# A hybrid attention and state-space layer: padded key tiles, wider tap and sample visits, a sample's keys as 96 + 96 + 80 rows

## The chip, the cores and the metric

The kernel runs as one program on one core of a Trainium2 chip. The metric is the device time in microseconds (us) of one execution, from a program that is launched once; lower is better. The core has five engines that run their own instruction streams and meet at semaphores: TensorE (PE in the profile, with its weight loads apart as PEld), VectorE (DVE), ScalarE (ACT), GpSimd (POOL) and SyncE (SP), which here issues all the transfers, on one queue in order.

## What is computed

One layer works on 512 new rows of a prompt and on 8 running streams ("samples") of 16 new rows each, with 256 cached keys a stream. Both branches read the same normed input through one combined projection; cut to what matters here:

```python
h = rmsnorm(x, g) @ w_in                       # 640 rows x 1024, w_in 1024 x 8192
q, k, v, ga, u, gs, gl = split(h)
# attention: 8 heads, two softmax maps a head, q/k 64 wide, v 128 wide
s = einsum('bqmhd,bkmhd->bmhqk', q, k) - slopes * |q_pos - k_pos|     (masked by chunks of 64)
p = softmax(s);  w = p[:, 0] - lam * p[:, 1]
o = einsum('bhqk,bkhe->bqhe', w, v)            # samples: keys = 256 cached + 16 new
ya = (rmsnorm(o) * silu(ga)) @ w_attn_proj
# S5 state space: 64 groups of 16 channels, 64 complex states a group
hr, hi = associative_scan(a, b @ u)            # h[t] = a h[t-1] + b u[t], along the rows
ys = gelu(Re(c h) + d u);  ys = ys * sigmoid(ys @ w_glu + b_glu)
ys = (ys * silu(gs)) @ w_ssm_proj
y = x + (sigmoid(g_a) * ya + sigmoid(g_s) * ys) @ w_out
```

The new keys and values, and the last states, are outputs too.

## The kernel before, in words

Nearly all instructions are recorded at line 222, where `Meter.go` calls the engine; the rows are therefore told apart by the names of their tiles.

**The main line** is 4032 products into the banks `ps_mm`, in the order of the table `ORDER`: vA, u, kA, ga, qA, gs, kB, qB, vB, the rest of gs, xa, xs, then ap, gl, sp, o0 and o1. Each fp32 operand is split into a high and a low part of a faster type, and a product is done as hi x hi, hi x lo and lo x hi (`mm3`). Weights come in as `wraw` tiles of 512 KB and are split by ACT (`whi`) and DVE (`wlo`). Half A of the keys and queries serves heads 0 to 3, half B heads 4 to 7.

**Side work** is written as generators. The class `Weave` keeps a modelled clock of every engine, and puts the next step of a generator between two products of the main line when it expects its inputs to be there. This fixes PE's order at build time (`manual_schedule` for TensorE); the other engines' orders come from a list scheduler with its own model. On the chip every engine works in that order and waits at semaphores. A run of such instructions between two `ps_mm` products is called a visit here.

The side work that the change touches, in the order in which it runs:

- `ssm_tap`: for each of 16 blocks of four groups, DVE or POOL builds a table `E` and PE makes four products of 32 columns of the array (`ps_pv<-E,bbs`) into one bank. ACT and DVE evacuate it to `tap`, and SP writes it to `tap_d` in DRAM.
- `attend`: 16 steps for each half, four tiles of 128 queries by four heads, two score maps each, so 64 maps. A map is two products into `ps_s`: `kT,qT` on 128 rows (the query's hi and lo rows against the key's hi rows, which stand twice), and `kTl,qT` on the 64 rows of the head (the query's hi rows against the key's lo rows). All heads of a half share the tile `kTl`, one head of a pair in its rows 0 to 63, the other in rows 64 to 127. Then come transposes of the weights `sb` and products with the values (`ps_pv<-vt,wth` and `wtl`).
- `states`: the recurrence over chunks, in two parts of 45 and 44 columns through one buffer `R`. A part is loaded from `s_d` (4 transfers), runs step by step (four operations a step, `m`, `m`, `m`, `R`, on POOL or, in some steps, on DVE), and is stored to `r_d` (4 transfers). The second part cannot be loaded before the first is stored. `states` starts after the last tap (`after("tap")`), because its pool takes the taps' place, and its end (`after("states")`) opens the pool of the samples' scores.
- `evac_k` and `evac_q` norm the rows of keys and queries. The root (`rs`) is done on POOL, between the steps of `states`; PE transposes the result (`ps_tp<-ident,kn`), and DVE and ACT split it.
- `sample_setup`, `sample_k`, `sample_scores`: after `states`, the samples' cached keys `skt` (512 KB each, `KH` = 2 buffers) and the queries `qk` are loaded, `prep` copies the queries into the block-diagonal tiles `qbd`, and each sample gets two visits of four products of 32 columns (`ps_s<-skt,qbd`), one for each map.
- `sample_v`, `sample_pv`: the weights of a sample are transposed in pieces of 128, 128 and 16 keys, and multiplied with two value tiles `svt` (`VH` = 4 buffers) and a small one, `svn`, of 16 new rows.

`director` starts these in turn; the state-space outputs (`out_load` to `out_gelu`) and the last products follow.

Of the kernel before, what the change touches and what calls it, by code (L numbers as in the profile page):

```python
# [10 lines left out]
F32 = mybir.dt.float32  # L11
# [20 lines left out]
# columns of the packed parameters  # L32
# [27 lines left out]
    # of the two engines for plain arithmetic, the one with less to do  # L60
# [7 lines left out]
    # when the last part of what is read is there  # L68
# [9 lines left out]
    # when the n-th next tile of the tag has its place  # L78
# [4 lines left out]
    # when the place of a tile is free  # L83
# [34 lines left out]
    # the step goes on when its loads are there  # L118
# [70 lines left out]
class Meter:  # L189
    """An engine whose instructions are counted at their expected price."""  # L190
# [4 lines left out]
    def __getattr__(self, op):  # L195
        fn = getattr(self.e, op)

        def go(out, *args, **kw):
# [36 lines left out]
def trunk(nc, tc, a):  # L235
# [24 lines left out]
    # when the n-th result of the name is expected; with placed, as soon as its instructions are in  # L260
# [15 lines left out]
    # ---------------------------------------------------------------- helpers  # L276
# [22 lines left out]
    # when the n-th next bank is free  # L299
# [5 lines left out]
    # ---------------------------------------------------------------- DRAM scratch  # L305
# [5 lines left out]
    qk_d = [dram.tile([128, 8, 2, 2, 32], F32, name=f"qk_d{i}") for i in range(2)]   # row, sample, map, half  # L311
# [5 lines left out]
    # ---------------------------------------------------------------- constants  # L317
# [6 lines left out]
    isl = pers.tile([128, 2, 8], F32, name="isl")       # one over the slopes, by half, map and head  # L324
# [5 lines left out]
    # operands of the products: hi and lo parts, by k  # L330
# [6 lines left out]
    # ---------------------------------------------------------------- products  # L337
# [15 lines left out]
    # the transfers run two ahead of the splitting  # L353
# [1262 lines left out]
```

## Time and profile before

| what | value |
|---|---|
| three runs | 911.86, 914.41, 915.0 us; median 914.41 |
| profiled execution, span | 910.4 us (its own time is not listed apart) |
| PE | 874.9 us busy, 96% of the span |
| PEld | 778.4 us, 85% |
| DVE | 561.4 us, 62% |
| ACT | 377.8 us, 41% |
| POOL | 258.1 us, 28% |
| DMA | 165.78 MB, mean 182 GB/s |
| mean granted TensorE clock | 0.979 of full speed |

A row of a timeline gives start, duration, engine, operation with its tiles, shape and count, and in brackets the idle time before it with the one that ended it. A PE row's duration is from issue to result, and products overlap, so what a product costs PE is the distance from its start to the next start. For `64*128 64x384` read: 64 rows and 128 columns of the array, 384 elements streamed.

### The profile page before, as it was taken

The page shows a single profiled execution, that of the slowest core. Times are in us where ns is not written, and L with a number is a line of the kernel's source. Part 1 is how long each engine was busy: PE and PEld are TensorE (multiplying, and loading weights), DVE is VectorE, ACT ScalarE, POOL GpSimd, SP SyncE. Part 2 cuts the span into 40 slices and gives each one's busy share as a digit, 9 for nine tenths or more (in the row PEclk, how much of TensorE's full clock was granted, in tenths as well). Part 3 has the DMA queues.
Part 4 walks back from the last instruction along what each step waited for, and adds up shares of the span by engine and source line. Part 5 has one row for each costly group of instructions (what it writes and reads, how often), then busy time and mean ns, then how long its engine had stood idle before and what let it go on. Part 6 is the DMA issues. An engine that isn't in the chain of part 4 may idle for free.

```text
span 910.4 us, 15615 instructions
## 1 busy us (share of the span) xinstructions
PE 874.9 (96%) x5692; PEld 778.4 (85%) x5692; DVE 561.4 (62%) x1263; ACT 377.8 (41%) x796; POOL 258.1 (28%) x428
## 2 busy tenths in 40 slices
PE   8999998999999999789999999999899999999998
PEld 6898978899778788577777797889899999999986
DVE  6689278987596874467668843323577755565421
ACT  6332244554265443144556543433465644432110
POOL 2843076661124971497822110000000000000000
PEclk8999998999999999799999999999999999999999
DMA  8265647767439339553387579955989754345331
GB/s 297 98 204 160 199 143 216 232 209 237 125 105 200 100 97 142 122 163 92 104 151 261 162 257 356 352 186 177 278 239 306 259 205 154 99 130 173 105 126 58
DMA packets 145437, 165.78 MB, mean 182 GB/s; under 512 B 49104, under 2 KB 109136, under 8 KB 145360
## 3 DMA queue, kind: packets, MB, share of 16 engines
q1 hardware_dynamic: 145360, 164.78, 60.5%
q8 instruction: 45, 0.74, 0.3%
q14 instruction: 32, 0.26, 0.1%
HBM read 117.63 MB, written 42.93 MB: 176 GB/s over the span
## 4 chain that ended last, share of the span: by engine, by line
PE 69%; DMA 10%; DVE 9%; POOL 6%; issue 3%; ACT 2%; SPq 1%; ACTq 0%; DVEq 0%; POOLq 0%
PE ps_mm L222 55%; PE ps_s L222 7%; PE ps_tp L222 4%; PE ps_pv L222 3%; DMA wraw<-in_wb_dram 3%; POOL m L222 2%; DMA T<-tap_d 2%; DVE wlo L222 2%; SPq L222 1%; DMA R<-s_d 1%; DMA r_d<-R 1%; POOL rs L222 1%; DMA Ef<-e_d 1%; POOL R L222 1%; POOL F L222 1%
## 5 line engine op out<-in xcount | busy, mean ns | idle before, releaser
L222 PE MATMUL ps_mm<-xh,whi 128*128 128x320 f32 x640 | 207.8, 325 | 2.1 <-DVE ue L222 2.1
L222 PE MATMUL ps_mm<-xh,wlo 128*128 128x320 f32 x640 | 200.4, 313 | 0.0
L222 PE MATMUL ps_mm<-xl,whi 128*128 128x320 f32 x640 | 200.2, 313 | 0.0
L222 DVE TENSOR_TENSOR wlo<-wraw,whi 128x1024 fp32r<-128x1024 f32 x96 | 119.7, 1248 | 80.8 <-ACT whi L222 79.8
L222 ACT ACTIVATE whi<-wraw 128x1024 fp32r<-128x1024 f32 x96 | 101.6, 1059 | 123.7 <-PE ps_mm L222 94.7
L222 PEld LDWEIGHTS ps_mm<-xh,whi 128*128 128x128 f32 x640 | 122.8, 192 | 11.7 <-issue 8.6
L222 PEld LDWEIGHTS ps_mm<-xl,whi 128*128 128x128 f32 x640 | 122.9, 192 | 0.2
L222 PEld LDWEIGHTS ps_mm<-xh,wlo 128*128 128x128 f32 x640 | 122.5, 191 | 0.0
L222 PE MATMUL ps_mm<-whi,xh 128*128 128x512 f32 x240 | 100.6, 419 | 1.1 <-ACT xh L222 1.1
L222 PE MATMUL ps_mm<-wlo,xh 128*128 128x512 f32 x240 | 96.0, 400 | 0.0
L222 PE MATMUL ps_mm<-whi,xl 128*128 128x512 f32 x240 | 95.8, 399 | 0.0
L222 POOL TENSOR_TENSOR m<-a,R 128x64 f32<-128x64 f32 (+1 forms) x128 | 55.1, 455 | 13.6 <-DMA R<-s_d 6.5
L222 PEld LDWEIGHTS ps_mm<-whi,xh 128*128 128x128 f32 x240 | 46.5, 194 | 11.7 <-issue 1.4
L222 PEld LDWEIGHTS ps_mm<-whi,xl 128*128 128x128 f32 x240 | 46.3, 193 | 10.6 <-DVE xl L222 0.3
L222 PEld LDWEIGHTS ps_mm<-wlo,xh 128*128 128x128 f32 x240 | 46.4, 194 | 8.8 <-DVE wlo L222 0.7
L222 POOL TENSOR_TENSOR rs<-ss,mhalf 128x8 f32<-128x8 f32 x20 | 33.5, 1674 | 55.4 <-DVE ss L222 51.8
L222 PE MATMUL ps_mm<-ogh,whi 128*128 128x320 f32 x128 | 41.3, 323 | 0.0
L222 PE MATMUL ps_mm<-ogh,wlo 128*128 128x320 f32 x128 | 40.0, 313 | 0.0
L222 PE MATMUL ps_mm<-ogl,whi 128*128 128x320 f32 x128 | 39.9, 312 | 0.0
L222 PE MATMUL ps_mm<-yh,whi 128*128 128x320 f32 x128 | 39.6, 309 | 0.0
L222 PE MATMUL ps_mm<-yh,wlo 128*128 128x320 f32 x128 | 39.6, 309 | 0.0
L222 PE MATMUL ps_mm<-y2h,whi 128*128 128x320 f32 x128 | 39.6, 309 | 0.0
(291 smaller groups left out, 1897.0 us busy)
## 6 DMA issues: line engine op xcount, KB each, us to landing
wraw<-in_wb_dram SPq DMA_DIRECT2D x64, 512.0 KB
wraw<-in_wa_dram SPq DMA_DIRECT2D x32, 512.0 KB
u<-u_d SPq DMA_DIRECT2D x16, 640.0 KB
skt<-in_ckt_dram SPq DMA_DIRECT2D x16, 512.0 KB
svt<-in_cv_dram SPq DMA_DIRECT2D x16, 512.0 KB
u_d<-ue SPq DMA_DIRECT2D x8, 640.0 KB
gate_xa<-gate SPq DMA_DIRECT2D x16, 320.0 KB
e_d<-E SPq DMA_DIRECT2D x16, 256.0 KB
```

Of the source, the lines that this page charges most:

```text
L222: r = fn(out, *args, **kw)
```

## The change

Four parts. (a) The lo product of a score map is done on all 128 rows, with one lo tile for each head of a pair, whose other 64 rows are zero; POOL clears these rows, two memsets of 64 x 2048 in each half. (b) The taps of four blocks are built first, and then done in one visit of 16 products into one bank of 512 columns, with one evacuation by ACT. (c) The two score maps of a sample are done in one visit, with `KH` = 4 key buffers. (d) A sample's 272 keys are cut into 96, 96 and 80 rows; the last tile takes 64 cached and the 16 new ones, with `VH` = 6 buffers. All comments are gone too, and the program is built with `dynamic_dma_scratch_size=256`. The diff, cut to the core:

```diff
@@ ssm_tap
+        tpz = tpe.tile([128, TB, 240], F32, name="tap")
-            E = tpe.tile(sh, F32, name="E", tag="E", bufs=1)
+                E = tpe.tile(sh, F32, name="E", tag="E", bufs=TB)
...
-            yield room("pv")
+                yield room("pv") if b == b0 + TB - 1 else None
             pt = ps_pv()
-            for g in range(4):
-                PE.matmul(pt[g * 32:g * 32 + 32, :128], bbs[:, 4 * b + g:4 * b + g + 2, :].rearrange("p g n -> p (g n)"),
-                          Ef[:, g, :128], start=True, stop=True)
-            AC.activation(tp, pt[:, :128], AF.Copy)
+            for i, Ef in enumerate(Efs):
+                for g in range(4):
+                    gb = 4 * (b0 + i) + g
+                    PE.matmul(pt[g * 32:g * 32 + 32, i * 128:i * 128 + 128],
+                              bbs[:, gb:gb + 2, :].rearrange("p g n -> p (g n)"), Ef[:, g, :128], start=True, stop=True)
+            AC.activation(tp, pt[:, :TB * 128].rearrange("p (b c) -> p b c", b=TB), AF.Copy)
...
+            for i in range(TB):
+                SP.dma_start(tap_d[b0 + i].rearrange("n g c -> g n c"), tpz[:, i, :])
@@ evac_k
-                KT[hf] = [atk.tile([128, 4, 512], F32R, name=f"kT{x}", tag="kT", bufs=3) for x in "01l"]
+                KT[hf] = [atk.tile([128, 4, 512], F32R, name=f"kT{x}", tag="kT", bufs=4) for x in ("0", "1", "l0", "l1")]
+            if t == 0:
+                for h2 in range(2):
+                    PL.memset(f(KT[hf][2 + h2][HALVES[1 - h2]]), 0.0)
...
-                    split(d[own, :, ts], KT[hf][2][own, :, ts], pt[own])
+                    split(d[own, :, ts], KT[hf][2 + h2][own, :, ts], pt[own])
@@ attend
-            PE.matmul(ps[:, :nk], q[rows, j, :], kl[rows, j, :nk], start=False, stop=True)
+            PE.matmul(ps[:, :nk], q[:, j, :], kl[:, j, :nk], start=False, stop=True)
@@ sample_v
-        for x in range(16):
-            b, j = divmod(x, 2)
+        for x in range(24):
+            b, j = divmod(x, 3)
+            n = 96 if j < 2 else 64
+            SP.dma_start(v[:n], a["cv"][b, j * 96:j * 96 + n, :])
+            if j == 2:
+                SP.dma_start(v[64:80], v_d[b * 16:b * 16 + 16])
@@ sample_scores
+            yield Free(both(after("kh", 2 * b + 2), after("qbd", b + 1), room("s", 2)))
+            pss = [ps_s(), ps_s()]
             for m in range(2):
-                yield Free(both(after("kh", 2 * b + m + 1), after("qbd", b + 1), room("s")))
...
-                W.give("kh")
+            W.give("kh", 2)
@@ sample_pv
-            for j in range(2):
-                PE.transpose(ps[:, j * 128:(j + 1) * 128], w[:, j * 128:(j + 1) * 128], ident)
-            PE.transpose(ps[:16, 256:384], w[:, 256:272], ident)
+            for j, n in enumerate(VROWS):
+                PE.transpose(ps[:n, j * 128:(j + 1) * 128], w[:, j * 96:j * 96 + n], ident)
...
-            for j, x in enumerate((wt[:, 0], wt[:, 1], wn)):
+            for j, n in enumerate(VROWS):
                 v = VS.pop((b, j))
@@ constants
+VROWS = 96, 96, 80
+TB = 4
-KH = 2
-VH = 4
+KH = 4
+VH = 6
```

The planner and the scheduler answer to this with other orders. On POOL, where `states` passes from its first part to its second (`last` holds the column between them; `osc` and `rs` are roots for norms; kTl are the new lo tiles), the order before is:

```order
L222 TENSOR_TENSOR R<-R,m_4164 128x64
L222 COPY last<-R 128x64
L222 COPY R<-last 128x64
L222 TENSOR_TENSOR m_4321<-a_111,R 128x64
L222 TENSOR_TENSOR m_4322<-a_111,R 128x64
L222 TENSOR_TENSOR m_4321<-m_4321,m_4322 128x64
L222 TENSOR_TENSOR osc<-oss,mhalf 128x4
L222 TENSOR_TENSOR R<-R,m_4321 128x64
L222 TENSOR_TENSOR m_4327<-a_111,R 128x64
L222 TENSOR_TENSOR m_4328<-a_111,R 128x64
L222 TENSOR_TENSOR rs<-ss,mhalf 128x8
```

and with the change, with the two memsets some 20 rows further up, inside the first part:

```order
L222 TENSOR_TENSOR osc<-oss,mhalf 128x4
L222 TENSOR_TENSOR m_3986<-m_3986,m_3987 128x64
L222 MEMSET kTl_4344 64x2048
L222 MEMSET kTl_4345 64x2048
L222 TENSOR_TENSOR R<-R,m_3986 128x64
...
L222 COPY last<-R 128x64
L222 TENSOR_TENSOR osc<-oss,mhalf 128x4
L222 COPY R<-last 128x64
L222 TENSOR_TENSOR m_4256<-a_111,R 128x64
L222 TENSOR_TENSOR m_4257<-a_111,R 128x64
L222 TENSOR_TENSOR m_4256<-m_4256,m_4257 128x64
L222 TENSOR_TENSOR rs<-ss,mhalf 128x8
```

The first `rs` of half B moved from behind the first step that needs the loaded `R` to ahead of it, and the memsets of half B stand among the steps of `states`.

On SP's queue, where the samples' loads are issued once `states` is done (`skt` is 512 KB; `qk<-qk_d_70` are the queries, `qk<-qk_d_71` the new keys), the order before is:

```order
L222 DMA bias_s<-in_bias_s_dram 128x272
L222 DMA qk<-qk_d_71 128x128
L222 DMA skt<-in_ckt_dram 128x4x256 x2
L222 DMA qk<-qk_d_70 128x128 x2
L222 DMA v_d<-v 128x512
```

and with the change:

```order
L222 DMA bias_s<-in_bias_s_dram 128x272
L222 DMA qk<-qk_d_71 128x128
L222 DMA skt<-in_ckt_dram 128x4x256 x2
L222 DMA qk<-qk_d_71 128x128
L222 DMA skt<-in_ckt_dram 128x4x256 x2
L222 DMA qk<-qk_d_70 128x128 x2
```

The first queries stand behind four key loads in place of two.

On PE, the first visit of the samples' scores, before (ahead of it are 1906 products of the main line):

```order
L222 MATMUL ps_mm<-xh_94,whi 128x320
L222 MATMUL ps_mm<-xl_96,whi 128x320
L222 MATMUL ps_mm<-xh_94,wlo 128x320
L222 MATMUL ps_s<-skt,qbd_5501 32x272 x4
L222 MATMUL ps_pv<-vt,wth 128x256
L222 MATMUL ps_pv<-vt,wtl 128x128
```

and with the change (ahead of it are 1870):

```order
L222 MATMUL ps_pv<-vt,wth 128x256
L222 MATMUL ps_pv<-vt,wtl 128x128
L222 MATMUL ps_s<-skt,qbd_5330 32x272 x8
L222 MATMUL ps_mm<-xh_94,whi 128x320
L222 MATMUL ps_mm<-xl_96,whi 128x320
```

The visit holds eight products in place of four, and it stands 36 main products earlier. On the same engine the transposes of half B's second key tile moved from the place behind 1576 main products to that behind 1558.

## Rows read from the trace of the kernel before

**Rows 1.** The page: busy time by engine, and the chain by engine.

```profile
PE 874.9 (96%) x5692; PEld 778.4 (85%) x5692; DVE 561.4 (62%) x1263; ACT 377.8 (41%) x796; POOL 258.1 (28%) x428
...
PE 69%; DMA 10%; DVE 9%; POOL 6%; issue 3%; ACT 2%; SPq 1%; ACTq 0%; DVEq 0%; POOLq 0%
```

**Rows 2.** Timeline of PE, two score maps: start, us, operation.

```profile
301.92 0.39 PE L222 MATMUL ps_s<-kT,qT 128*128 128x384 f32 x1
302.24 0.44 PE L222 MATMUL ps_s<-kTl,qT 64*128 64x384 f32 x1
302.61 0.44 PE L222 MATMUL ps_s<-kT,qT 128*128 128x384 f32 x1
```

**Rows 3.** Timeline of PE, a visit of taps.

```profile
263.28 0.40 PE L222 MATMUL ps_mm<-whi,xl 128*128 128x512 f32 x1
263.60 0.42 PE L222 MATMUL ps_pv<-E,bbs 128*32 128x128 f32 x8
263.96 0.50 PE L222 MATMUL ps_mm<-whi,xh 128*128 128x512 f32 x1
264.30 0.40 PE L222 MATMUL ps_mm<-wlo,xh 128*128 128x512 f32 x1
264.54 0.40 PE L222 MATMUL ps_mm<-whi,xl 128*128 128x512 f32 x1
```

**Rows 4.** Timeline of PE, two visits of sample scores.

```profile
518.85 1.12 PE L222 MATMUL ps_s<-skt,qbd 128*32 128x272 f32 x16
519.90 0.42 PE L222 MATMUL ps_mm<-xh,whi 128*128 128x320 f32 x1
...
524.04 0.67 PE L222 MATMUL ps_s<-skt,qbd 128*32 128x272 f32 x8
524.64 0.41 PE L222 MATMUL ps_mm<-xh,whi 128*128 128x320 f32 x1
```

**Rows 5.** PE's waits: us in total, times, longest.

```profile
PE ps_tp L222 <- DVE kn L222: 9.0, 2, 6.7
```

**Rows 6.** Timeline of POOL, the chain of the states.

```profile
287.09 0.66 POOL L222 TENSOR_TENSOR m<-a,R 128x64 f32<-128x64 f32 x2 [6.52 <-DMA R<-s_d]
...
331.01 1.01 POOL L222 TENSOR_TENSOR osc<-oss,mhalf 128x4 f32<-128x4 f32 x1 [3.46 <-DVE oss L222]
...
357.03 0.30 POOL L222 COPY R<-last 128x64 f32<-128x64 f32 x1 [14.76 <-DMA r_d<-R]
...
371.50 0.35 POOL L222 TENSOR_TENSOR R<-R,m 128x64 f32<-128x64 f32 x1 [12.04 <-DMA R<-s_d]
...
372.55 1.64 POOL L222 TENSOR_TENSOR rs<-ss,mhalf 128x8 f32<-128x8 f32 x1
```

**Rows 7.** Timeline of SP, the first part's loads.

```profile
273.92 2.10 SPq L222 DMA_DIRECT2D qT<-ql  x1
...
279.25 0.57 SPq L222 DMA_DIRECT2D R<-s_d  x1
```

**Rows 8.** Groups of POOL: memsets by shape.

```profile
L222 POOL MEMSET qbd<- 128x256 f32 x2 | 0.6, 312 | 12.7 <-DMA r_d<-R 12.7
...
L222 POOL MEMSET tap<- 128x112 f32 x1 | 0.2, 185 | 0.0
```

**Rows 9.** Timeline of SP, the samples' loads.

```profile
476.82 1.28 SPq L222 DMA_DIRECT2D skt<-in_ckt_dram  x2
478.15 1.13 SPq L222 DMA_DIRECT2D qk<-qk_d  x2
```

**Rows 10.** Timeline of POOL, the samples' queries.

```profile
484.51 1.32 POOL L222 COPY qbd<-qk 64x128 f32<-64x128 f32 x4 [3.34 <-DMA qk<-qk_d]
```

**Rows 11.** Timeline of PE, where the score visit will stand.

```profile
480.22 0.36 PE L222 MATMUL ps_mm<-xh,whi 128*128 128x320 f32 x1
...
488.10 0.67 PE L222 MATMUL ps_s<-skt,qbd 128*32 128x272 f32 x8
```

**Rows 12.** Windows around PE's longest wait (PEclk is granted clock).

```profile
376.00:382.00 6.00, 6.00 (x17) 4.91 (x18) 4.66 (x12) 1.18 (x2) 3.82 (x7) 0.52 0.31 87
```

More of the change, by code (lines that the diff above doesn't have):

```diff
@@ L746, in ssm_tap @@
         PL.memset(bbs[:, 64], 0.0)
-        tpz = tpe.tile([128, 240], F32, name="tap")
-        PL.memset(tpz[:, :112], 0.0)
-        tp = tpz[:, 112:]
-        for b in range(16):
-            g4 = slice(4 * b, 4 * b + 4)
-            sh = [128, 4, 9, 16]
-            cc = tpe.tile([128, 2, 4, 16], F32, name="cc", tag="cc", bufs=2)
-            SP.dma_start(cc, a["cC"][b].rearrange("p r (g n) -> p r g n", n=16))
-            W.hold()
-            E = tpe.tile(sh, F32, name="E", tag="E", bufs=1)
-            Et = tpe.tile(sh, F32, name="Et", tag="Et", bufs=1)
-            en = W.lighter()
-            en.tensor_tensor(E, P1[:, g4, :, None].to_broadcast(sh), cc[:, 0, :, None, :].to_broadcast(sh), op=OP.mult)
-            en.tensor_tensor(Et, P2[:, g4, :, None].to_broadcast(sh), cc[:, 1, :, None, :].to_broadcast(sh), op=OP.mult)
-            en.tensor_tensor(E, E, Et, op=OP.add)
-            Ef = E.rearrange("p g j n -> p g (j n)")
-            SP.dma_start(e_d[:, g4, :], Ef[:, :, 16:])
-            yield room("pv")
-            pt = ps_pv()
-            for g in range(4):
-                PE.matmul(pt[g * 32:g * 32 + 32, :128], bbs[:, 4 * b + g:4 * b + g + 2, :].rearrange("p g n -> p (g n)"),
-                          Ef[:, g, :128], start=True, stop=True)
-            AC.activation(tp, pt[:, :128], AF.Copy)
-            DV.scalar_tensor_tensor(tp[:, :16], dm, dT[:, b:b + 1], tp[:, :16], op0=OP.mult, op1=OP.add)
-            SP.dma_start(tap_d[b].rearrange("n g c -> g n c"), tpz)
@@ new lines, in ssm_tap @@
+        tpz = tpe.tile([128, TB, 240], F32, name="tap")
+        PL.memset(tpz[:, :, :112], 0.0)
+        tp = tpz[:, :, 112:]
+        sh = [128, 4, 9, 16]
+        for b0 in range(0, 16, TB):
+            Efs = []
+            for b in range(b0, b0 + TB):
+                g4 = slice(4 * b, 4 * b + 4)
+                cc = tpe.tile([128, 2, 4, 16], F32, name="cc", tag="cc", bufs=2)
+                SP.dma_start(cc, a["cC"][b].rearrange("p r (g n) -> p r g n", n=16))
+                W.hold()
+                E = tpe.tile(sh, F32, name="E", tag="E", bufs=TB)
+                Et = tpe.tile(sh, F32, name="Et", tag="Et", bufs=1)
+                en = W.lighter()
+                en.tensor_tensor(E, P1[:, g4, :, None].to_broadcast(sh), cc[:, 0, :, None, :].to_broadcast(sh), op=OP.mult)
+                en.tensor_tensor(Et, P2[:, g4, :, None].to_broadcast(sh), cc[:, 1, :, None, :].to_broadcast(sh), op=OP.mult)
+                en.tensor_tensor(E, E, Et, op=OP.add)
+                Efs.append(E.rearrange("p g j n -> p g (j n)"))
+                SP.dma_start(e_d[:, g4, :], Efs[-1][:, :, 16:])
+                yield room("pv") if b == b0 + TB - 1 else None
+            pt = ps_pv()
+            for i, Ef in enumerate(Efs):
[5 more added lines that the diff above has]
+            for i in range(TB):
+                DV.scalar_tensor_tensor(tp[:, i, :16], dm, dT[:, b0 + i:b0 + i + 1], tp[:, i, :16], op0=OP.mult, op1=OP.add)
+            for i in range(TB):
+                SP.dma_start(tap_d[b0 + i].rearrange("n g c -> g n c"), tpz[:, i, :])
@@ L936, in attend @@
         hp, h2 = divmod(h4, 2)
-        rows = HALVES[h2]
-        q, kd, kl = QT[hf, t][h2], KT[hf][h2], KT[hf][2]
+        q, kd, kl = QT[hf, t][h2], KT[hf][h2], KT[hf][2 + h2]
         sb = at.tile([128, 512], F32, name="sb", tag="sb", bufs=SB)
@@ L1114, in sample_v @@
     def sample_v(sm):
[L1115 to L1116 removed]
+        for x in range(24):
+            b, j = divmod(x, 3)
             yield Free(W.has("vh"))
             W.take("vh")
[L1119 to L1123 removed]
+            n = 96 if j < 2 else 64
+            v = VS[b, j] = sm.tile([128, 1024], F32, name="svt", tag="svt", bufs=VH)
+            SP.dma_start(v[:n], a["cv"][b, j * 96:j * 96 + n, :])
+            if j == 2:
+                SP.dma_start(v[64:80], v_d[b * 16:b * 16 + 16])
             W.hold()
@@ L1146, in sample_scores @@
             mx, z = small(sm, "smx", 2), small(sm, "sz", 2)
+            yield Free(both(after("kh", 2 * b + 2), after("qbd", b + 1), room("s", 2)))
+            pss = [ps_s(), ps_s()]
             for m in range(2):
-                yield Free(both(after("kh", 2 * b + m + 1), after("qbd", b + 1), room("s")))
                 kt = KS.pop((b, m))
-                ps = ps_s()
                 for hp in range(4):
-                    PE.matmul(ps[hp * 32:hp * 32 + 32, :272], S["qbd"][b % 2][:, m, hp, :], kt[:, hp, :],
+                    PE.matmul(pss[m][hp * 32:hp * 32 + 32, :272], S["qbd"][b % 2][:, m, hp, :], kt[:, hp, :],
                               start=True, stop=True)
-                W.give("kh")
-                if m == 0 and b < 7:
-                    prep(b + 1)
-                DV.tensor_tensor_reduce(p[:, m, :], ps[:, :272], bias_s, scale=1.0, scalar=3.0e38,
+            W.give("kh", 2)
+            if b < 7:
+                prep(b + 1)
+            for m in range(2):
+                DV.tensor_tensor_reduce(p[:, m, :], pss[m][:, :272], bias_s, scale=1.0, scalar=3.0e38,
                                         op0=OP.add, op1=OP.min, accum_out=mx[:, m:m + 1])
@@ L1591, in build @@
 def build(shapes):
-    nc = bacc.Bacc("TRN2", target_bir_lowering=False, num_devices=1)
+    nc = bacc.Bacc("TRN2", target_bir_lowering=False, num_devices=1, dynamic_dma_scratch_size=256)
     a = {}
```

18 lines of the change are left out of this document (6 added, 12 removed).

## The prediction, made blind

> **What bounds the kernel now.** I read the page first, then PE's waits, then the timelines around what they named. PE is busy for 96% of the span and has 69% of the chain that ended last [rows 1], so time that PE is spared is time of the kernel, as long as nothing else takes the place. Of its waits one is large: the transposes of half B's normed keys wait 9.0 us in two times, 6.7 in the longest [rows 5]. The timeline of POOL tells what that is: the chain of the states. It starts its first step at 287.09, when the loads of R land, goes on to a transfer out and back (waits of 14.76 and 12.04 us), and takes up its second part at 371.50; the root `rs` for the keys stands behind that wait and starts at 372.55 [rows 6]. The chain goes on at 371.50 and ends in the loads of the samples, whose last piece, the copies of the queries, begins at 484.51 and takes 1.32 us [rows 10]: the samples can be scored from 485.8. PE came to that visit at 488.10 [rows 11], so it did not wait for it; the slack was 2.3 us. **Up to here two chains run side by side, PE's and the states', and they end almost together.** That is what the forecast rests on.
>
> **What PE is spared.** A score map takes 302.61 - 301.92 = 0.69 us for two products of 384 columns [rows 2]. A product of 512 columns among its like is 0.24 from the next, 264.30 to 264.54 [rows 3], so 384 columns would take 0.18 and the map 0.36. The 0.33 on top are paid where 128 rows change to 64 (0.32 to the next start) and back (0.37), and I take them as equal at every width, since they stand for a change and not for columns: 64 x 0.33 = 21 us. With zeros in the other 64 rows all of it goes. The zeros cost PE nothing, as time goes by columns.
>
> The rule on this is the Trainium skill, TensorEngine Tiling (Array Packing), Key Properties: a change of tiling mode drains the engine. The rows agree, and by that rule alone the sum would be all of PE's saving, the first rival below.
>
> A visit of taps is entered in 0.32 and left in 0.34, against 0.24 [rows 3]: 0.18 us. A single map of sample scores takes 524.64 - 524.04 = 0.60, two in a row 519.90 - 518.85 = 1.05 [rows 4], so the second costs 0.45 and 0.15 are paid once. Both together make 0.33 a visit. The taps go from 16 visits to 4: 12 x 0.33 = 4.0. Of the 14 visits of scores (two hold both maps already) 8 stay: 6 x 0.33 = 2.0. In the value products the last piece has 80 rows where it had 16, one change less and back in each of 8 visits: half of a map's price, 0.17, at most 1.4 and I take 1.0. PE's sum is 21 + 4 + 2 + 1 = 28 us.
>
> **When it is spared, and what is late next.** Of the 64 maps 52 stand ahead of the first score visit in its new place: 52 x 0.33 = 17.2, with the taps' 4.0, come before it; 12 x 0.33 = 4.0 of maps, the 2.0 and the 1.0 come behind it. PE passed that place at 480.22 [rows 11], with no wait for the samples. It would now be there near 459, and must wait for the end of the states' chain, in two places: at the second key tile of half B, whose `rs` still stands behind the loads of R (the first `rs` is now ahead of them, and helps only that tile), and at the first scores. So the time up to this visit is the chain's, and I sum that one:
>
> - Start. The last taps are done earlier by their own 4.0, less the last visit's share, by 6 products of 0.24, and by a map or two: some 6 us. The loads of R then stood behind query transfers on SP, one of 2.10 us at 273.92, with the last load issued only at 279.25 [rows 7] and its step 7.8 later [rows 6]. With the change the queries of the first three tiles go ahead of the tap writes, the last tile's behind the loads. I take -9 for both, between -5 (the queries' waits come back ahead of the tap writes, in order on the same queue) and -12.
> - Memsets. Half A's stand at the program's start, where POOL waits for the first norms, and cost nothing. Half B's are in the chain. By 312 ns for 256 columns and 185 for 112 [rows 8] a column is 0.88 ns, so 2048 take 1.9 us: an estimate of +3.8 for two, between 0 (if they fall into a wait of POOL) and 3.8.
> - The `osc` that made POOL wait 3.46 us in the first part [rows 6] now has a like behind `last`, where POOL waits for the transfer anyway. Between -3.5 and 0; I take -2.5.
> - The second part itself: its roots wait for PE's keys, and PE now runs at the same distance from it or nearer; 12 steps go to DVE in place of 8. Between -5 and +5; nothing, as the signs oppose.
> - The sample loads. Two key loads and the queries behind them took from 476.82 [rows 9] to 484.51 [rows 10], 7.7 us. Two more key loads of 512 KB now stand ahead of the queries: between 0 and 7.7; with PE waiting, fewer weights are asked for at that time, and I take +3.4.
>
> Together -4.3: ready at 481.5, and PE scores at 481.8, **1.6 later than it passed this place before**. Then the clock. In the 6 us behind the wait of [rows 5] PE worked at a granted 0.52 [rows 12], the level of 1.2 GHz in place of 2.4: 2.9 us lost. That loss stays with the wait for the keys, and a second long wait adds another like it: +2.5, between 0 and 2.9. The Trainium skill, TensorE: Matmul & The Clock Gate, says the same of idle time, that it throttles the engine, and this row agrees.
>
> Behind the visit the gains are kept, as nothing waits on PE there for long: -4.0 - 2.0 - 1.0 = -7.0. The values' loads for the first product may come late, since `svt` is issued behind a key load that waits for a later score visit: +0.5, between 0 and 2. The rest of the added work is covered: DVE's four small tap operations in place of four of 128 columns are the same count, and ACT's evacuation of 512 columns replaces four.
>
> Sum: +1.6 + 2.5 - 7.0 + 0.5 = **-2.4 us, to a span of 908.0.** The profiled span of 910.4 is 4.0 below the median of the runs, so 912.0 there.
>
> **The rivals.**
>
> 1. PE's saving is kept whole. This needs the states' chain to move forward as far as PE does, for instance if most of its second part was waiting for PE's keys. For it: PE has 69% of the chain [rows 1], and the changes' price is plain in the rows. Against it: from R's landing to 371.50 the chain waits for transfers and for its own steps, which PE does not set. It gives 910.4 - 28 = 882, so 886 as a median. Chance 0.13.
> 2. The chain gains more than I sum: the start at -12, the osc at -3.5, the key loads at +1. Ready at 485.8 - 12 + 3.8 - 3.5 + 1 = 475.1, PE scores 4.8 earlier than it passed, and -4.8 + 2 - 7 + 0.5 = -9.3: 905 as a median, in a stretch of 899 to 909. For it: the queries are out of R's way, and the loads run while little else does. Chance 0.27.
> 3. Slower: the scores become ready late. The start gains only 5, since SP is held by six query transfers ahead of the last tap writes; the memsets cost 3.8; the queries wait for all of the two more key loads, 7.7. Ready at 485.8 - 5 + 3.8 + 7.7 = 492.3, PE scores 12.4 later than it passed, and 12.4 + 2.5 - 7 + 0.5 = +8.4: 923. It decides against the change from the point where the scores are ready later than 483.9 (then the lateness, 4.0, and the 3.0 of clock and values eat the 7.0). Against it: POOL's first step waits for R's landing, and PE brings the last taps earlier in any case. Chance 0.23, in a stretch of 915 to 926.
> 4. The 0.33 of a map is not the change of rows but belongs to reading the half-height tile or to the accumulation. Then the product on 128 rows costs as before, the 21 us stay where they were, and the waits hardly grow: the chain of the sum ends 1.6 late only if PE is early, so PE's own line decides, at -4 -2 -1 = -7, with +3.8 of memsets in a chain that was 2.3 from deciding: about -4 in all, 910. Chance 0.05.
>
> **How the numbers follow.** The forecast has 0.32 and its own stretch is 908 to 917. A measurement of this kernel tells about 0.3%, 2.7 us, from no change, and the forecast lies at that edge: of its 0.32 I count 0.12 as faster, 0.15 as same and 0.05 as slower. Rival 1 is faster, rival 2 all but 0.03, rival 3 slower but for 0.05, rival 4 faster by 0.03. That is 0.52 faster, with 0.25 same and 0.23 slower. The range goes from 897, below rival 2, to 924, above rival 3's middle: it leaves out rival 1 and the far end of rival 3, together some 0.18.
>
> **What would show it.** Map pairs with starts about 0.18 apart at 384 columns show the price of the change of rows; rival 4 falls by them. A wait of PE at the transposes of the second half B key tile, of about 10 us, and a wait of some 20 before the first `ps_s<-skt,qbd`, released by the samples' loads or by POOL, show the step on which the forecast rests; without them, rival 1. The first step of the states near 278, two memsets of 1.9 us inside the first part, and the queries' copies near 480 to 483 show the chain's terms one by one. PE at half clock behind each wait shows the +2.5. The forecast is wrong if the copies of the queries begin far from 480, or if PE is held by something that I do not have here, such as DVE between 250 and 275.

## The result, and the profile after

The changed kernel takes 960.94 us (median of 4 runs, 958.02 to 967.98), beside 914.70 of the kernel before: a ratio of 1.0527, with a 95% interval of 1.048 to 1.0574. The forecast was 912, with a range of 897 to 924; the time lies 37 us above its upper end. Ratios, here and below, compare runs in the faster of the chip's two states alone, and differ by up to 0.6% from the quotient of the two medians. The profiled execution has a span of 966.2, against 910.4; it is the slowest of the four, so the traces lie 55.8 us apart and the medians 46.2.

The page of the changed kernel, span and busy times, answers to [rows 1]:

```profile
span 966.2 us, 15564 instructions
...
PE 862.6 (89%) x5692; PEld 786.5 (81%) x5692; DVE 565.7 (59%) x1282; ACT 373.6 (39%) x784; POOL 256.6 (27%) x413
```

TensorE is busy for 12 us less and stands idle far more. The rows of its waits (us in total, times, longest) add up to 31.2 us before and 99.5 after. The largest of them, to be held against [rows 5] (`issue` is time in which no wait shows):

```profile
PE ps_s L222 <- POOL qbd L222: 24.7, 1, 24.7
PE ps_tp L222 <- DVE kn L222: 12.8, 5, 6.7
PE ps_tp L222 <- DVE sb L222: 9.2, 5, 6.5
PE ps_s L222 <- issue: 7.9, 3, 4.1
PE ps_s L222 <- DVE so L222: 6.8, 6, 2.1
PE ps_tp L222 <- DVE osm L222: 5.2, 1, 5.2
```

One wait of 24.7 us is the one that the forecast named, the first sample scores, released by the copies of the queries. The other rows are small ones of many kinds, and they are most of the difference.

Where the time goes can be read by counting main products. The table is worked out from the trace: the start of the n-th product of the main line before, and how much later (+) or earlier it starts in the changed kernel and in some experiments that follow.

| product | before, us | changed | `nudge_pool` | `a_pure` | `b_pure` | `b2_pure` | `ac_gap` |
|---|---|---|---|---|---|---|---|
| 480 | 100.4 | +5.2 | -0.2 | +0.7 | +3.0 | +1.4 | +1.2 |
| 960 | 221.7 | +14.3 | +7.0 | +3.6 | +10.7 | +2.3 | +3.4 |
| 1120 | 265.8 | +19.4 | +9.1 | +4.0 | +16.4 | +3.1 | +1.4 |
| 1360 | 334.1 | +26.1 | +16.5 | -1.8 | +25.3 | +4.7 | -8.8 |
| 1840 | 476.0 | +18.2 | +13.3 | -1.8 | +24.5 | +3.9 | -12.6 |
| 1920 | 497.7 | +42.4 | +26.2 | +4.2 | +24.3 | +3.4 | -8.6 |
| 2640 | 646.3 | +60.2 | +25.8 | +3.3 | +24.3 | +3.4 | -9.2 |
| 4000 | 899.3 | +55.7 | +25.9 | +4.0 | +25.7 | +4.7 | -12.5 |

The changed kernel is 14 us late at product 960, where not one score map has been done; 12 us more come between 960 and 1360; 24 at the first sample scores; 18 between 1920 and 2640. It wins 8 back between 1360 and 1840, and 4 to 5 behind 2640. From 3040 on both run level.

The saving itself is there. Two maps of 384 columns in the changed kernel (start, us) answer to [rows 2]:

```profile
332.25 0.33 PE L222 MATMUL ps_s<-kTl,qT 128*128 128x384 f32 x1
332.43 0.34 PE L222 MATMUL ps_s<-kT,qT 128*128 128x384 f32 x1
332.60 0.34 PE L222 MATMUL ps_s<-kTl,qT 128*128 128x384 f32 x1
332.78 0.31 PE L222 MATMUL ps_mm<-xh,whi 128*128 128x320 f32 x1
```

The lo product (`kTl`) starts 0.17 behind the hi product and the next hi product 0.18 behind it, in place of 0.32 and 0.37.

The chain of the states, on POOL, answers to [rows 6, 10] (rows of the first part's start, the memsets, the ends of both parts, the landing of the second, the queries' copies):

```profile
306.64 0.67 POOL L222 TENSOR_TENSOR m<-a,R 128x64 f32<-128x64 f32 x2 [2.60 <-DMA h<-in_h_dram]
...
355.99 3.66 POOL L222 MEMSET kTl<- 64x2048 f32 x2
...
367.64 0.30 POOL L222 COPY last<-R 128x64 f32<-128x64 f32 x1
...
397.61 0.36 POOL L222 TENSOR_TENSOR R<-R,m 128x64 f32<-128x64 f32 x1 [8.07 <-DMA R<-s_d]
...
495.71 0.29 POOL L222 COPY last<-R 128x64 f32<-128x64 f32 x1
...
522.42 1.32 POOL L222 COPY qbd<-qk 64x128 f32<-64x128 f32 x4 [3.00 <-DMA qk<-qk_d]
```

It starts 19.5 us later than before, not 9 earlier. SP's queue ahead of it, against [rows 7]:

```profile
255.59 9.28 SPq L222 DMA_DIRECT2D e_d<-E  x2
264.96 15.40 SPq L222 DMA_DIRECT2D qT<-ql  x6
281.21 2.43 SPq L222 DMA_DIRECT2D tap_d<-tap  x4
...
295.49 4.71 SPq L222 DMA_DIRECT2D R<-s_d  x2
```

SP waits 8.4 us of the first row for POOL, which builds the tap table `E` that is stored there; the six query transfers behind it take 15.4 us, as four of them wait again. TensorE waits 4.5 us for one of them (`qT<-ql`, in the view of waits). The last four tap writes stand behind the queries, but those do not hold them: the taps are made only then. TensorE's last visit of taps, and the four additions on DVE that finish them:

```profile
278.93 1.08 PE L222 MATMUL ps_pv<-E,bbs 128*32 128x128 f32 x32 [0.39 <-DVE o L222]
```

```profile
280.96 0.67 DVE L222 SCALAR_TENSOR_TENSOR tap<-dm,dT,tap 128x16 f32<-128x16 f32 x4
```

The first addition ends at 281.19, and its tap goes out at 281.21. Before, the last visit began at 263.60 [rows 3], 15.3 us earlier. At the other end the sample loads answer to [rows 9]:

```profile
512.49 1.28 SPq L222 DMA_DIRECT2D skt<-in_ckt_dram  x2
...
514.47 1.22 SPq L222 DMA_DIRECT2D skt<-in_ckt_dram  x2
515.74 8.34 SPq L222 DMA_DIRECT2D qk<-qk_d  x6
```

and TensorE's visit to [rows 11]:

```profile
523.11 2.04 PE L222 MATMUL ps_s<-skt,qbd 128*32 128x272 f32 x16 [24.70 <-POOL qbd L222]
```

### The profile page after: what moved, and what is told of

Its sections match the earlier page's. It is cut to its first block, busy times and chain, and to the rows that moved or that the text cites. A ratio compares the mean times of both kernels' runs of the same rounds, so it can differ in the third digit from the quotient of the medians.

```text
span 966.2 us, 15564 instructions
## 1 busy us (share of the span) xinstructions
PE 862.6 (89%) x5692; PEld 786.5 (81%) x5692; DVE 565.7 (59%) x1282; ACT 373.6 (39%) x784; POOL 256.6 (27%) x413
## 5 line engine op out<-in xcount | busy, mean ns | idle before, releaser
L222 PE MATMUL ps_mm<-xl,whi 128*128 128x320 f32 x640 | 203.1, 317 | 0.0
L222 PE MATMUL ps_mm<-xh,wlo 128*128 128x320 f32 x640 | 202.9, 317 | 0.0
L222 PEld LDWEIGHTS ps_mm<-xh,whi 128*128 128x128 f32 x640 | 125.7, 196 | 10.9 <-DVE ue L222 5.3
L222 PEld LDWEIGHTS ps_mm<-xl,whi 128*128 128x128 f32 x640 | 125.7, 196 | 0.4
L222 PEld LDWEIGHTS ps_mm<-xh,wlo 128*128 128x128 f32 x640 | 125.0, 195 | 0.0
L222 PE MATMUL ps_mm<-whi,xh 128*128 128x512 f32 x240 | 99.5, 415 | 1.0 <-ACT xh L222 1.0
L222 POOL TENSOR_TENSOR m<-a,R 128x64 f32<-128x64 f32 (+1 forms) x120 | 48.0, 423 | 16.0 <-DVE R L222 10.3
L222 PE MATMUL ps_mm<-y2h,wlo 128*128 128x320 f32 x128 | 39.6, 309 | 0.0
L222 PE MATMUL ps_mm<-yl,whi 128*128 128x320 f32 x128 | 39.6, 309 | 0.0
```

The lines of the kernel that those rows point to most:

```text
L222: r = fn(out, *args, **kw)
```

## The experiments

All parts of the change were put on and taken off one by one, and two things were held apart that the change moves together: what an operation does, and the order that the planner makes when its numbers shift. `..._pure` means that TensorE's instructions stand in the order of the kernel before, but for the visits that the part itself merges; the orders of the other engines shift with the part. Times are medians; each ratio is against the kernel before on the same chip, and chips differ between the groups of runs.

| run | us | before | ratio, 95% interval |
|---|---|---|---|
| `only_a`: padded key tiles | 932.89 | 913.97 | 1.0165 (1.0093 to 1.0237) |
| `only_b`: taps in fours | 940.74 | 913.97 | 1.0249 (1.0179 to 1.0320) |
| `only_c`: scores two to a visit | 912.59 | 913.97 | 0.9965 (0.9922 to 1.0007) |
| `only_d`: 96, 96 and 80 rows | 928.73 | 913.97 | 1.0114 (1.0063 to 1.0164) |
| `a_pure` | 916.86 | 917.33 | 0.9981 (0.9940 to 1.0023) |
| `nudge_pool` | 940.01 | 917.33 | 1.0192 (1.0110 to 1.0273) |
| `only_a_64` | 944.74 | 917.33 | 1.0257 (1.0154 to 1.0359) |
| `nudge_2us` | 934.93 | 917.59 | 1.0168 (1.0073 to 1.0262) |
| `b_pure` | 934.37 | 914.12 | 1.0244 (1.0173 to 1.0315) |
| `b_cc` | 928.01 | 917.59 | 1.0116 (1.0038 to 1.0194) |
| `b2_pure` | 916.70 | 914.90 | 1.0020 (0.9979 to 1.0061) |
| `d_two` | 926.54 | 914.12 | 1.0150 (1.0078 to 1.0221) |
| `all_pure` | 943.90 | 914.12 | 1.0351 (1.0289 to 1.0413) |
| `abc_cc` | 925.89 | 917.59 | 1.0089 (1.0053 to 1.0125) |
| `ac_pure` | 911.05 | 914.12 | 0.9973 (0.9931 to 1.0016) |
| `ac_gap` | 901.49 | 914.90 | 0.9832 (0.9753 to 0.9911) |
| `ac_gap_64` | 914.84 | 915.13 | 0.9975 (0.9934 to 1.0017) |
| `before_gap` | 924.63 | 915.13 | 1.0068 (1.0027 to 1.0109) |

One caution for the profiles: those of `only_c`, `only_d` and `d_two` lost some 10 us between products 1200 and 1320, where their order on TensorE and on DVE is that of the kernel before, while the times of that kernel itself ran from 908 to 929; a loss of one profile in that place is not read as the edit's.

### The parts, one at a time

`only_a`: the diff of `evac_k` and `attend` alone.

> Only the padded key tiles (part a) on the kernel before. Theory T (the taps in fours are what makes the kernel late: the states' chain then starts 20 us later): without them the ssm stage is as before, the chain starts near 287, and the kernel comes out at 900 to 912, the maps' 0.33 each showing as 0.18 a product. Rival S (each part costs by itself, through the order that the planner makes of it): 920 to 935 here as well. Rival M (the two memsets inside the states' chain make the scores late): 915 to 925, with a wait of PE at the first sample scores.

`only_b`: the diff of `ssm_tap` alone.

> Only the taps in fours (part b). T: the loss is nearly whole here: PE some 15 us late by product 1040, the states' first step near 305 in place of 287, a wait of PE at the first sample scores; 935 to 955. S: a part of it, 920 to 930. If taps in fours cost nothing: 908 to 914.

`only_c`: the diff of `sample_scores` and `KH` alone.

> Only the scores two maps to a visit and four key buffers (part c). T: near the kernel before, 910 to 918; a few us late if the queries behind four key loads are what the scores wait for. S: 920 to 935.

`only_d`: the diff of `sample_v`, `sample_pv` and `VH` alone.

> Only the samples' keys as 96, 96 and 80 rows (part d); the order up to the sample values is the one before. T: the waits for svt seen in the changed kernel (5.6 us with the new rows' loads) come from this part, so 915 to 922. S: the same number. If those waits were only a following of the late start: 912 to 915.

The four ratios add up to +1.65 + 2.49 - 0.35 + 1.14 = +4.9%, beside +5.3% for the whole. So three parts lose each by itself, and only the merged scores cost nothing. By the ranges that were set, `only_a` came out as rival S said and `only_b` and `only_c` as theory T did, while `only_d` lies above both. T, by which the taps are nearly all of it, falls by `only_a`: it loses without them, and its states' chain starts at 315.51, not near 287.

### Padded tiles: the operation or the order?

`a_pure` allocates the two lo tiles once, and clears them outside the planner's account; TensorE's order stays that of the kernel before.

```diff
+    KL = [atk.tile([128, 4, 512], F32R, name=f"kTl{x}") for x in "01"]
+    for h2 in range(2):
+        nc.gpsimd.memset(f(KL[h2][HALVES[1 - h2]]), 0.0)
...
-            if t == 0:
-                for h2 in range(2):
-                    PL.memset(f(KT[hf][2 + h2][HALVES[1 - h2]]), 0.0)
```

> The padded lo tiles alone, with TensorE's instructions in the order of the kernel before: the two tiles are allocated and cleared once, at the program's start, and the planner is not told of the two memsets. Theory S (the parts lose by the order that the planner makes when its numbers shift, not by what they do): the maps' 0.33 comes back as far as the states' chain lets it, some 6 us behind the first score visit and 2 before, so 900 to 910. Rival M (the products on 128 rows or the cleared tiles cost something themselves): 915 or more.

`nudge_pool` adds one line to the kernel before, and no instruction:

```diff
+            if t == 0:
+                W.busy["PL"] = max(W.busy.get("PL", 0.0), W.clock) + 4.1
```

> The kernel before, with not one instruction more: only the planner's clock of POOL is moved up by 4.1 us at each half's first key tile, which gives TensorE the very order that the padded tiles alone gave. S: as slow as the padded tiles alone or slower, as the maps save nothing here: 928 to 945, with the same 12 us lost by product 960. M: as the kernel before, 908 to 916.

`only_a_64` is `only_a` with one line back; all engines keep its order:

```diff
-            PE.matmul(ps[:, :nk], q[:, j, :], kl[:, j, :nk], start=False, stop=True)
+            PE.matmul(ps[:, :nk], q[rows, j, :], kl[rows, j, :nk], start=False, stop=True)
```

> The padded tiles alone, in the same order of every engine, but the lo product reads its own 64 rows as before. Against the padded tiles alone this shows what the 128 rows bring in that order. S: 4 to 15 us slower than those, as the waits eat the rest of the 21. If the change of rows cost nothing: the same time.

`nudge_2us` is the same nudge with 2.0.

> The kernel before with the planner's clock of POOL moved up by 2.0 us in place of 4.1 at each half's first key tile: no instruction more, a third order of TensorE (442 rows of difference from the kernel before, 408 from the order at 4.1). If the kernel before stands on a good order among many: slower here too, 925 to 945. If the order at 4.1 was a bad one: 908 to 918.

Two nudges without an instruction lose 1.9 and 1.7%. TensorE's order in `nudge_pool` is that of `only_a`, instruction by instruction. With this order and the old product the loss is 2.6%, with the new product 1.65%: the 128 rows bring 0.9%, about 8 us, though the two intervals overlap. In the order of the kernel before they bring nothing that can be measured. `a_pure` so misses theory S's 900 to 910 and lies in the range of rival M; but M's price of the products themselves does not fit the rows of the maps above. The trace of `a_pure` says where the 21 us are. TensorE's waits there (us in total, times, longest):

```profile
PE ps_tp L222 <- DVE kn L222: 6.8, 3, 4.1
PE ps_tp L222 <- DVE o L222: 5.6, 1, 5.6
PE ps_s L222 <- DVE mx L222: 5.2, 1, 5.2
...
PE ps_pv L222 <- ACT wth L222: 4.9, 1, 4.9
```

The rows of all its waits add up to 51.7 us, against 31.2 before: 20 more (3.7 of it at the program's start, where the identity tile now stands behind the two memsets on POOL, a cost of this way of clearing them). TensorE's busy time falls by 15.9 us, from 874.9 to 859.0, and 46 us of it lie at a granted 1.2 GHz in place of 26, by the trace's clock records behind the program's start. TensorE now comes to the attention's steps before DVE and ACT have the row maxima, the sums and the weights ready. So the padded tiles' loss is the order's, and in the old order their gain goes into waits, most of them in the attention, for DVE and ACT, and into the lower clock that follows waits.

### Taps in fours: the order, the small loads, or the pieces?

`b_pure` charges the planner for 16 visits of four products, and issues 16 products at each fourth place.

> The taps in fours, with TensorE in the order of the kernel before: the planner counts 16 visits of four products where they were, and their 16 products are issued at each fourth place. Theory S (the order that the planner makes of shifted numbers is what loses): 910 to 920, with the states' first step near 287. Rival G (grouping itself loses, since a tap's tables and its results now wait for three others, on DVE, POOL and SP): 930 to 942 as with the taps in fours alone.

The loss is whole in that order too, so it is not TensorE's order; rival G's range holds. The waits for the small table loads, in the window from 80 to 300 us, before on DVE, and in `only_b` on DVE and on POOL:

```profile
DVE E L222 <- DMA cc<-in_cC_dram: 0.9, 1, 0.9
```

```profile
DVE E L222 <- DMA cc<-in_cC_dram: 7.2, 2, 6.8
```

```profile
POOL E L222 <- DMA cc<-in_cC_dram: 4.4, 2, 3.6
```

11.6 us in place of 0.9: with one buffer for `E`, each block's load came while the block before waited for its visit; with four, the blocks are built one behind the other, and each load of `cc` is waited for with everything that is queued behind (so I read the code and these rows).

`b_cc` loads all of `cc` in one transfer ahead of the first table, in TensorE's order of `b_pure`:

```diff
-            cc = tpe.tile([128, 2, 4, 16], F32, name="cc", tag="cc", bufs=2)
-            SP.dma_start(cc, a["cC"][b].rearrange("p r (g n) -> p r g n", n=16))
+            cc = ccs[:, b]
```

> The taps in fours in TensorE's order of the kernel before, with the 16 small loads of `cc` replaced by one transfer at the start. Theory C (grouping loses because the tables are now built one behind the other, each behind its own load of 6 us, and DVE and POOL stand with everything queued behind: 10 us of such waits against 0.9 before): 910 to 920, PE level with the kernel before at product 960. Rival T (it loses through the tables' work itself, which now meets that of F, or through the tap writes that stand behind the queries on SP's queue): 925 to 940, still 10 us late at product 960.

About half of it is left: 1.0116, in the range of rival T, and the profile, that of the slowest of the four runs, is late at product 960 as before. It is +14.7 there, and +6.2 already at product 480, by a wait of 6.1 us for `ue` that ends at 79.4; the 1 MB transfer is issued only at 84.8, so this is not its doing, and the cause stays open. So theory C covers part of the loss at most. What is left can be read around 205 to 217 us of `b_cc`, first on DVE, then on POOL, then the product on TensorE that waited:

```profile
205.55 1.27 DVE L222 TENSOR_TENSOR F<-F,Ft 128x512 f32<-128x512 f32 x1
206.75 3.62 DVE L222 TENSOR_TENSOR E<-P,ccs 128x576 f32<-128x576 f32 x2
210.29 2.75 DVE L790 SCALAR_TENSOR_TENSOR tap<-dm,dT,tap 128x16 f32<-128x16 f32 x4
212.96 0.60 DVE L222 SCALAR_TENSOR_TENSOR so<-ps_s,sgn,so 128x128 f32<-128x128 f32 x2
```

```profile
207.81 1.94 POOL L222 TENSOR_TENSOR E<-E,Et 128x576 f32<-128x576 f32 x1
...
211.46 1.39 POOL L222 TENSOR_TENSOR E<-E,Et 128x576 f32<-128x576 f32 x1
```

```profile
217.20 0.47 PE L222 MATMUL ps_s<-u,Wh 128*128 128x160 f32 x1 [7.79 <-DVE so L222]
```

The `so` evacuation, for which the products of `ssm_in` wait, stands behind two table products (3.62 us) and four tap additions (2.75). In the kernel before one tap addition stands there:

```profile
198.90 0.68 DVE L222 TENSOR_TENSOR F<-F,Ft 128x512 f32<-128x512 f32 x1
199.50 1.14 DVE L222 SCALAR_TENSOR_TENSOR tap<-dm,dT,tap 128x16 f32<-128x16 f32 x1
200.56 0.60 DVE L222 SCALAR_TENSOR_TENSOR so<-ps_s,sgn,so 128x128 f32<-128x128 f32 x2
```

TensorE's waits for `so` between 80 and 300 us, before, in `b_cc`, and in the next run, which groups two blocks:

```profile
PE ps_s L222 <- DVE so L222: 1.8, 3, 1.0
```

```profile
PE ps_s L222 <- DVE so L222: 11.1, 4, 7.8
```

```profile
PE ps_s L222 <- DVE so L222: 4.3, 4, 1.7
```

`b2_pure` groups two blocks, in the same manner as `b_pure`.

> The taps in twos, with TensorE in the order of the kernel before (8 visits in place of 4 or 16), each block with its own load of cc. Theory Q (a group's tables and tap additions run in one piece on DVE, and the so evacuations that TensorE waits for stand behind them, so the loss grows with the group): about half of that of the fours, 918 to 926, some 4 to 7 us late at product 960. Rival N (any disturbance of the other engines' orders costs about the same): 928 to 938.

In twos the loss is gone (1.0020, and 2.3 us late at product 960 in place of 10.7), more than theory Q gave: the size of the group, not any disturbance, is what costs, and the loss grows faster than it. In between nothing was tried. That the loss comes by way of the queue on DVE is read from these rows; no run held the pieces there apart from the loads and the other orders.

### Sample values

`d_two` loads the first 192 cached rows of a sample in one transfer.

> The samples' keys as 96, 96 and 80 rows alone, but with the first 192 rows of a sample in one transfer, so three transfers a sample as before in place of four, and the same bytes. If the loss of this part is the number of transfers (each transfer of SP's queue waits for an earlier one to land): 912 to 917, and the waits of PE for the samples' keys go. Rival: the values' products or the order cost it: 920 to 930 as before this edit.

It does not help (1.0150, within the interval of `only_d`), so the number of transfers is not it. In `only_d` TensorE waits for the samples' keys, which it did not before, and in `d_two` for less but still:

```profile
PE ps_s L222 <- DMA skt<-in_ckt_dram: 6.3, 3, 5.4
```

```profile
PE ps_s L222 <- DMA skt<-in_ckt_dram: 2.9, 2, 2.3
```

The key loads stand behind the values on SP's queue, and SP waits there for transfers of `svt`: 22.1 us in `only_d` between 490 and 720 us, 21.6 in `d_two`, 10.6 before. Why these waits are longer in this form stays open; the 1% was not taken apart further.

### Together, and a faster version

`all_pure`: padded tiles and taps as in `a_pure` and `b_pure`, the scores two to a visit, the values as in `d_two`.

> All four parts, the padded tiles and the taps in TensorE's order of the kernel before, the sample values with three transfers a sample. S: the four operations themselves lose nothing, 905 to 918, in place of 961. Rival G: 930 or more.

`abc_cc`: the same without the sample values, and `cc` in four loads, each a group ahead.

> Three parts of the change (padded tiles, taps in fours, scores two to a visit) in TensorE's order of the kernel before, `cc` in four transfers, each a group ahead; the sample values as before. C: 904 to 916. T: 925 to 940.

Of the changed kernel's 5.3%, 3.5% are left in `all_pure`, about the sum of the taps' and the values' parts (2.4 and 1.5); 0.9% in `abc_cc`. Both missed their expectations under S and C, and came out as rivals G and T said.

`ac_pure`: padded tiles as in `a_pure`, and the scores two to a visit.

> The padded tiles in the order of the kernel before, and the scores two maps to a visit. Each alone came out level with the kernel before, the second 0.35% below it within its interval. If their savings add where no wait takes them (behind the first score visit): 902 to 910. If every saving goes into waits: 912 to 917.

Level, between the two ranges. As TensorE now waits for DVE and ACT in the attention, the planner was told to leave more room:

```diff
-GAPS = 1.3, 0.8, 0.4, 0.2
+GAPS = 1.3, 1.2, 0.4, 0.2
```

`ac_gap` is `ac_pure` with this line.

> The padded tiles and the scores two to a visit, which were 0.3% below the kernel before, with the planner told to leave 1.2 us in place of 0.8 between a result and its use in the attention stage, as TensorE there now waits for DVE and ACT (mx, o, wth). If these waits come from placing the steps too early: 896 to 908. If any new order loses against the one before: 918 to 935.

901.49 us, a ratio of 0.9832: below both kernels. The waits for `mx`, `wth` and `sb` are no longer among its largest:

```profile
PE ps_tp L222 <- DVE oss L222: 7.8, 1, 7.8
PE ps_tp L222 <- DVE gaT L222: 5.7, 1, 5.7
...
PE ps_s L222 <- DVE so L222: 3.6, 4, 1.9
PE ps_tp L222 <- DVE kn L222: 3.0, 3, 1.6
```

`before_gap` is the kernel before with this line alone.

> The kernel before with the gap of the attention stage at 1.2 us in place of 0.8, and nothing else. If the gap alone makes the gain of the version that came out at 0.983 (padded tiles, scores two to a visit, this gap): 898 to 906. If it needs the padded tiles, since there PE runs ahead of DVE and ACT: 910 to 930.

`ac_gap_64` is `ac_gap`, the same order on every engine, with the lo product on 64 rows.

> The version that came out at 0.983, in the same order of every engine, with the lo product of a map back on its own 64 rows. This shows what the 128 rows bring in that order. If the saving is kept where PE no longer waits: 910 to 922, up to 21 us slower. If the order alone is the gain: 898 to 905.

The gap alone loses 0.7%, the order of `ac_gap` with the old product gains nothing that can be measured, and the 128 rows in it bring 0.9975 - 0.9832 = 1.4%, some 13 of the 21 us. The gain takes the padded tiles and the gap; what the merged scores add to it was not held apart.

## Why the prediction was wrong

- **Map price, 0.33 each.** Right in size: 0.17 and 0.18 between starts where 0.32 and 0.37 stood, so rival 4 falls. The visits' 0.33 is right too (0.33 for a merged tap visit in `b_pure`, 0.34 for a merged score visit in the changed kernel, worked out from the traces). What the maps' saving brings depends on the order around it: nothing in `a_pure`, about 8 us between `only_a_64` and `only_a`, 13 between `ac_gap_64` and `ac_gap`.
- **The step that failed: TensorE "would now be there near 459", with all its savings ahead of the first score visit, and only the states' chain to wait for.** It came there at 523.11 - 24.70 = 498.4, which is 18 later than before with 21 us less to do. I had read the saving as time that stays, because TensorE was 96% busy, and took every other engine's place as covered. The stage from 125 to 230 us, and the attention, are close-run between TensorE, DVE, ACT and POOL, in an order that the planner makes; a shift of 2 or 4 us in its account loses some 15 and 18 us by itself, and the rows that I had read say nothing of that. The prediction's own sign, PE "held by something that I do not have here", came true, and well ahead of the 250 to 275 us that it named (5.2 us late at product 480).
- **Start of the chain, -9.** It came out at +19.5 (306.64 against 287.09). It fails by the same step: TensorE's last visit of taps came 15.3 us later (278.93 against 263.60), where I had it 6 earlier. The other 4.2 lie between this visit and the first step, where four tap writes now go out in a row in place of one. Rival 3 had the six query transfers hold the tap writes, and let that cost 4 of the 9; the rows do not bear this out, as the first tap is written 0.02 us after DVE has finished it.
- **The taps' building, costed at nothing.** I counted their products and left out that four tables and four additions now run in one piece on engines that TensorE waits for. `b_pure` and `b2_pure` show what the grouping costs: 2.4% in fours, nothing in twos.
- **Chain terms.** Memsets: +3.8 estimated, 3.66 measured. First part as a whole: 61.0 us in place of 54.9; an `osc` there still makes POOL wait, 4.8 us for 3.5, so it gave nothing back. Second part, taken as nothing: 98.1 in place of 91.0; POOL waits in it for the keys' sums of squares (`ss`) 16.7 us in place of 6.9. From the last step to the copies' end: 28.0 in place of 23.3. Of these +4.7 only 2.0 lie behind the clearing of `qbd`, at 511.51 and 475.55, with the loads, where I took +3.4; 2.8 lie ahead of it, in the store of the second part. With the start and 0.5 of the transfers between the parts they make 19.5 + 6.1 + 0.5 + 7.1 + 4.7 = +37.9, and the copies end at 523.7 against 485.8. That the first scores wait for this chain was right, and is the 24.7 us. The wait at half B's second key tile came too, 6.7 us in place of about 10. By the traces its transposes stand behind 1548 main products, and stood behind 1542 before, so they moved 6 back; the section on the change has them 18 forward.
- **Clock, +2.5.** The granted clock of the wait and the stretch behind it, beside [rows 12] (columns as there):

```profile
500.00:523.00 23.00, 0.00 (x0) 0.00 (x0) 2.33 (x7) 0.43 (x1) 2.90 (x9) 0.52 1.09 226
523.00:527.00 4.00, 3.89 (x23) 2.52 (x24) 1.48 (x7) 1.23 (x4) 1.63 (x7) 0.50 0.43 101
```

  It is at the lower level, 1.2 GHz, as forecast. But the term was counted at one more wait, and many smaller ones have such a stretch behind them. By the clock records of the traces, behind the program's start, TensorE had 1.2 GHz for 92 us in the changed kernel and for 32 before, and was busy in 52 and 26 of them. At that level a product of 512 columns starts 0.43 behind the last (377.70 and 378.12 in the kernel before) and 0.23 at the upper one (364.82 and 365.05), so about half of the difference, 13 us, is an estimate of what the clock took in place of 2.5. `nudge_pool` bears it out, which has the products of the kernel before and is busy for 9.4 us more than its 874.9 [rows 1]:

```profile
PE 884.3 (94%) x5692; PEld 785.2 (84%) x5692; DVE 566.7 (61%) x1263; ACT 378.5 (40%) x796; POOL 261.2 (28%) x428
```

- **Behind the visit, -7.0.** It came out at +13: waits for the sample values (4.0 and 1.6 us in the view of waits), for the sample norms (5.2) and their stretches of lower clock. In `only_d`, too, TensorE falls 10 us further behind between products 1920 and 2640.
- **Chances.** 0.23 stood on slower, nearly all of it on a late states' chain (rival 3), and none on TensorE itself being late. The rules of the two pages of the Trainium skill that the prediction cites, on the change of mode and on idle time, agree with the rows (0.17 and 0.18 a product; a granted 0.52 in the wait of 24.7 us and 0.50 behind it). Neither says what the planner's order or the grouping costs.

## What to carry to other kernels

Where an order is made from modelled prices, a change alters the order as well as the operation, and the two must be priced apart: nudge the planner without an instruction, and keep the order with the new operation. A saving on the busiest engine comes back only where the others are ready for it; here it needed the planner's gap set anew (0.8 to 1.2 us) before 21 us of saved time gave 13. Many small waits cost more than their sum, as stretches of lower clock follow them. Small work that is gathered into larger pieces for one engine's sake must be looked at on the engines that prepare and take it up, in the queue in which something else waits.

## What was not expected of the hardware

The table product of 576 columns takes 0.75 us on DVE in most cases, but 1.66 at the longest before, and 3.62 for two in `b_cc`, while POOL ran the like (its own took 1.94 there, against 1.39 just behind). In `b_cc` five of nine take 1.07 to 1.97 us, and each of the five has operations of POOL beside it for 1.1 us or more, as has the one of 1.66 us before. The other eight there have POOL beside them for 0.2 us at most and take 0.75 to 0.80. One of 0.75 in `b_cc` has POOL beside it throughout, so company alone does not make it longer. The rows (duration in ns: least, median, most), before and in `b_cc`:

```profile
L222 DVE TENSOR_TENSOR E<-P,cc x9: 750/758/1657, 84.9 to 245.2; 128x576 f32<-128x576 f32 x9
```

```profile
L222 DVE TENSOR_TENSOR E<-P,ccs x9: 745/1069/1974, 93.7 to 247.5; 128x576 f32<-128x576 f32 x9
```

The Trainium skill, SBUF — State Buffer, in its section SBUF: two separate sides, says that a DVE operation with two inputs in SBUF and a GpSimd operation that reads SBUF lock each other out for whole instructions at a shared port. The rows agree with it so far: two of DVE's take 2.1 us more than twice 0.75, and the one of POOL's that runs across both takes 1.94. No run here takes the two engines apart. If it is so, gathered elementwise work is dearer than its sum when both engines are given it at once.
